# A gated attention and convolution block: ScalarE and TensorE handed to the scheduler behind the plain pairs, second-half operands emitted two products later

## The chip, the cores and the metric

The kernel runs on one core of one Trainium2 chip. The metric is the time of one execution on the device, in microseconds (us). An execution starts with all inputs in the chip's main memory and ends when the output stands there.

## What is computed

The input x is 2048 tokens by 1024 channels, float32, one layer:

```python
h    = rmsnorm(x, norm_g)
proj = h @ w_in                      # 1024 -> 6144 columns: q k v z_att B C u z_conv g_att g_conv
A    = attention(q, k, v, rel_bias)  # 8 heads of 64, own chunk of 64 and the 8 before it
ya   = (A * silu(z_att)) @ w_att_out
yc   = (B * conv3(C * u) * silu(z_conv)) @ w_conv_out
x    = x + (sigmoid(g_att) * ya + sigmoid(g_conv) * yc) @ w_out
out  = rmsnorm(x, final_norm_g)
```

## The kernel before

**Halves, pairs and products.** The projection is cut into two halves of 1024 tokens and, in each, 24 pairs of 128-column tiles. Most pairs are multiplied by a Strassen-like scheme: seven products of combined operands in place of eight, numbered 1 to 7 and taken in `ORDER` = 1, 2, 6, 5, 7, 4, 3 (line 35). Only the first half's first three pairs are multiplied plainly. The 21 pairs behind them make 147 products; this document counts them 0 to 146, and the second half's begin with 147. The last two pairs of the first half, A and B, are taken together in the order A1 A2 A6 B1 B2 B6 A5 B5 A7 B7 A4 B4 A3 B3 (products 133 to 146), the first two of the second half in the order 1 2 1 2 6 6 5 5 7 7 4 4 3 3 (products 147 to 160).

**One product.** Float32 precision comes from splitting each operand in a rounded part and its residual. A product is 12 matmuls of 128x128 by 128x512 into one PSUM bank (`passes`, lines 131 to 137): for each of four row blocks L135 (rounded weights, rounded tokens), L136 (rounded weights, token residual) and L137 (weight residual, rounded tokens). So the first matmul needs the rounded weights, and only the third needs the weight residual.

**Weights.** `operand(p, i)` makes the weights of a product: VectorE sums where the scheme wants them (L390 to L396), then `split_into`, a cast on ScalarE (L122) and the residual on VectorE (L123). The tile comes from a ring of four (`wr`), and in the first half each split weight is also stored to main memory on SyncE's queue (L399) for the second half to load (L381). A cast into a tile of the ring must wait until the product four back is done and its store has landed. `operand` is called two products ahead in the first half.

**Evictions.** Behind its matmuls a product's bank is read by VectorE (L746 to L766) or copied by ScalarE (L742), then what the pair is for follows: tanh and a store for gates (L404), a split for q and k (L410, L411), transposes on TensorE and a split for v (L433, L440, L441), SiLU for z (L453, L454). Three banks take turns.

**The second half's token operands.** `operand_steps(1)` makes them: seven steps, one for each operand number, each of four casts on ScalarE (L128, `t10h` is the rounded part of operand 1, row block 0) and four residuals on VectorE (L129), with VectorE sums ahead of some (L354, L356, L360). They go into the tiles of the first half's operands, so each step has to wait for product B of its number. In the loop a step follows product B of its number: `assert next(turned) == i` at the end of the iteration.

**What sets the order.** From the loop's start to product 160 the order of ScalarE and TensorE is the order of the program text (`tc.manual_schedule(engines=engines - {DVE})`, lines 700 and 701, closed at line 785). VectorE's order there, and every engine's later, is set by the framework's scheduler from the order in which the code emits instructions and its own estimates. Each engine then works through its instructions in that order, waiting on semaphores. DMA queues keep the order of the program.

## Time and profile before

| what | value |
|---|---|
| times of three runs | 1573.85, 1577.24 (median), 1580.59 us |
| the profiled execution | 1571.1 us, of which the profile's span is 1569.3 us |
| TensorE | busy 97% of the span |
| VectorE, ScalarE, GpSimd | 67%, 43%, 10% |
| chain that ended last | TensorE 62%, VectorE 4%, DMA 2%, ScalarE 1% |

The times of a row are microseconds from the span's start. A matmul's record is 0.39 us long though one starts every 0.23 us, since they are pipelined; what a wait costs is therefore read from starts of products. "Idle before" an instruction names what ended the wait.

### The profile page before, as it was taken

The numbers are of one execution on the slowest core, as the hardware profiler recorded it, in microseconds if no ns is written. First come the engines' busy times: TensorE is split into PE (matmuls) and PEld (weight loads), VectorE is DVE, ScalarE is ACT, GpSimd is POOL, SyncE is SP. The second block draws the span as 40 slices with busy tenths as digits, with TensorE's granted clock in tenths as the row PEclk, the third lists the DMA queues.
The fourth block names the chain that finished last, engine by engine and source line by source line (L and its number), as shares of the span: only waits on it lengthen the run. The fifth ranks groups of instructions, "written<-read, shape, count | busy, mean of one in ns | idle before, by whom it ended". The sixth has DMA issues, their size and how long they took to land.

```text
span 1569.3 us, 21720 instructions
## 1 busy us (share of the span) xinstructions
PE 1522.1 (97%) x7396; PEld 1268.2 (81%) x7396; DVE 1045.3 (67%) x2094; ACT 682.6 (43%) x1266; POOL 154.9 (10%) x294
## 2 busy tenths in 40 slices
PE   9899999999998999999999999999999999999997
PEld 6677878888786787888888888888887788888886
DVE  7978779797668653666565455446678786656544
ACT  6353343443335242333344444446666676523211
POOL 0000000000000001111121012012332222000000
PEclk9999999999999999999999999999999899999999
DMA  5287898989996926787899889898967668369231
GB/s 210 79 293 298 309 338 306 371 298 311 332 338 230 318 92 215 222 266 238 295 313 314 303 281 287 270 314 274 294 200 228 203 217 273 124 220 316 67 108 68
DMA packets 161711, 393.65 MB, mean 251 GB/s; under 512 B 20160, under 2 KB 40640, under 8 KB 161600
## 3 DMA queue, kind: packets, MB, share of 16 engines
q1 hardware_dynamic: 131392, 306.25, 56.2%
q0 software_dynamic: 20992, 69.22, 14.0%
q10 hardware_dynamic: 9216, 16.78, 2.9%
q8 instruction: 59, 0.97, 0.3%
q14 instruction: 52, 0.43, 0.1%
HBM read 241.18 MB, written 150.99 MB: 250 GB/s over the span
## 4 chain that ended last, share of the span: by engine, by line
PE 62%; DVE 4%; DMA 2%; ACT 1%; issue 1%; SPq 0%; DVEq 0%; ACTq 0%
PE ps_d L137 13%; PE ps_d L135 13%; PE ps_d L136 13%; PE ps_s L190 4%; PE po L228 4%; PE ps_d L873 3%; PE ps_d L875 3%; PE ps_d L874 3%; PE ps_t L210 3%; DMA wraw<-wy 1%; ACT pr L200 1%; DMA wraw<-wo 0%; DVE ps_s L196 0%; DVE ptl L216 0%; PE vt L433 0%
## 5 line engine op out<-in xcount | busy, mean ns | idle before, releaser
L158 POOL DMA_DIRECT2D q<-q x128 | 66.6, 526 | 710.4 <-DVE wc L123 603.3
L200 ACT ACTIVATE pr<-ps_s,nmax 128x640 f32<-128x640 f32 (+4 forms) x128 | 93.3, 729 | 89.8 <-DVE nmax L196 86.2
L196 DVE CUSTOM_DVE_ANT_0 ps_s<-ps_s,bs 128x640 f32<-128x640 f32 (+4 forms) x128 | 95.4, 745 | 48.1 <-PE ps_s L190 47.5
L215 ACT CAST pth<-ps_t 128x640 fp32r<-128x640 f32 (+4 forms) x128 | 79.8, 623 | 99.9 <-PE ps_t L210 98.5
L202 ACT ACTIVATE pr<-pr,rs 128x640 f32<-128x640 f32 (+4 forms) x128 | 97.7, 763 | 24.2 <-DVE rs L201 24.2
L190 PE MATMUL ps_s<-kk,q 128*128 128x320 f32 (+1 forms) x448 | 99.5, 336 | 8.5 <-ACT pr L200 8.3
L122 ACT CAST wc<-wraw 128x512 fp32r<-128x512 f32 x120 | 72.9, 619 | 76.5 <-DMA wc<-wc 41.6
L136 PE MATMUL ps_d<-mid,wy 128*128 128x512 f32 x256 | 101.4, 396 | 0.0
L135 PE MATMUL ps_d<-mid,wy 128*128 128x512 f32 x256 | 101.2, 395 | 0.0
L137 PE MATMUL ps_d<-mid,wy 128*128 128x512 f32 x256 | 101.2, 395 | 0.0
L216 DVE TENSOR_TENSOR ptl<-ps_t,pth 128x640 fp32r<-128x640 f32 (+4 forms) x128 | 94.2, 736 | 1.1 <-ACT pth L215 0.8
L123 DVE TENSOR_TENSOR wc<-wraw,wc 128x512 fp32r<-128x512 f32 x120 | 81.1, 688 | 12.5 <-ACT wc L122 11.5
L210 PE MATMUL ps_t<-ident,pr 128*128 128x128 f32 x560 | 84.2, 276 | 1.0 <-DVE ptl L216 0.8
L228 PE MATMUL po<-pth,vv 128*128 128x256 f32 x336 | 80.1, 272 | 2.3 <-ACT pth L215 2.2
L228 PE MATMUL po<-ptl,vv 128*128 128x256 f32 x336 | 78.5, 281 | 0.0
L190 PEld LDWEIGHTS ps_s<-kk,q 128*128 128x128 f32 x448 | 67.9, 191 | 13.0 <-ACT pr L200 12.3
L210 PEld LDWEIGHTS ps_t<-ident,pr 128*128 128x128 f32 x560 | 63.3, 140 | 11.1 <-issue 3.2
L228 PEld LDWEIGHTS po<-pth,vv 128*128 128x128 f32 x336 | 64.3, 191 | 6.8 <-ACT pth L215 3.4
L228 PEld LDWEIGHTS po<-ptl,vv 128*128 128x128 f32 x336 | 64.5, 192 | 2.7
L757 DVE TENSOR_TENSOR c<-v,ps_d 128x512 f32<-128x512 f32 x45 | 30.9, 687 | 48.7 <-PE ps_d L137 46.4
L884 ACT ACTIVATE sq<-y 128x512 f32<-128x512 f32 x32 | 20.2, 631 | 92.1 <-DVE y L879 92.0
L746 DVE TENSOR_TENSOR c<-u,ps_d 128x512 f32<-128x512 f32 x45 | 30.9, 686 | 42.3 <-PE ps_d L137 38.5
(370 smaller groups left out, 4260.0 us busy)
## 6 DMA issues: line engine op xcount, KB each, us to landing
wc<-wc SPq DMA_DIRECT2D x294, 512.0 KB, 4.7
wraw<-wp_in SPq DMA_DIRECT2D x54, 512.0 KB, 6.2
q<-q POOLq DMA_DIRECT2D x128, 128.0 KB, 4.9
gl<-gate SPq DMA_DIRECT2D x64, 256.0 KB, 3.9
mid<-mid SPq DMA_DIRECT2D x64, 256.0 KB, 5.7
bs<-bias POOLq DMA_DIRECT2D x32, 320.0 KB, 7.1
gate<-c ACTq DMA_DIRECT2D x34, 256.0 KB, 4.6
v<-vst SPq DMA_DIRECT2D x64, 128.0 KB, 4.6
```

The lines of the kernel that those rows point to most:

```text
L123: nc.vector.tensor_sub(w[:, 1], src, w[:, 0].bitcast(F32))
L135: nc.tensor.matmul(ps, lhsT=w[:, 0, k, :], rhs=rh[:, cs], start=(first and k == 0), stop=False)
L136: nc.tensor.matmul(ps, lhsT=w[:, 0, k, :], rhs=rl[:, cs], start=False, stop=False)
L137: nc.tensor.matmul(ps, lhsT=w[:, 1, k, :], rhs=rh[:, cs], start=False, stop=(last and k == len(rhs) - 1))
L190: nc.tensor.matmul(ps[:, i, :m], lhsT=q[s][:, g * P:(g + 1) * P], rhs=kk[:, k1 - n + i * m:k1 - n + (i + 1) * m], start=(s == 0), stop=(s ...
L196: nc.vector.tensor_tensor_reduce(out=view, in0=view, in1=bv, scale=-0.125, scalar=3.0e38, op0=ALU.add, op1=ALU.min, accum_out=nmax)
L200: nc.scalar.activation(out, view, AF.Exp, bias=nmax, scale=-1.0, accum_out=rs)
L202: nc.scalar.activation(pr[:, :n], pr[:, :n], AF.Identity, scale=rs)
L210: nc.tensor.transpose(out=ps[:, j * P:(j + 1) * P], in_=pr[:, j * P:(j + 1) * P], identity=ident)
L215: nc.scalar.copy(hi[:, js, qs], src)
L216: nc.vector.tensor_sub(lo[:, js, qs], src, hi[:, js, qs].bitcast(F32))
L228: nc.tensor.matmul(ps[:, (g0 + a) * P:(g0 + b) * P], lhsT=vv[:, g0 + j, :], rhs=s[:, j, a * P:b * P], start=(i == 0 and s is pt[0]), stop= ...
```

## The change

The manual order of ScalarE and TensorE behind the plain pairs is dropped, so that the scheduler orders them there as it orders VectorE. And a step of `operand_steps(1)` is no longer run at the end of the iteration s of its product B, but at the start of iteration s + 2, ahead of that iteration's weights: two products later. No arithmetic and no instruction is added or taken away.

```diff
--- before.py
+++ after.py
@@ -697,19 +697,21 @@
         scaled(*held0)
         for fn in late:
             fn()
-    manual = ExitStack()
-    manual.enter_context(tc.manual_schedule(engines=engines - {mybir.EngineType.DVE}))
     x1 = None
     nbias = 0
     att = None
     ab = None
     at_stages = 0
     turned = None
+    due = []
     uv = {}
 
     for s, (p, i) in enumerate(seq):
         half = p // NPAIR
         n = names.index(p)
+        if due and due[0] <= s:
+            due.pop(0)
+            next(turned)
         if half == 0 and i == 1 and n + 1 < NPAIR:
             for k in range(2):
                 load_raw(names[n + 1], k)
@@ -770,7 +772,7 @@
                 for _ in x1:
                     pass
                 turned = operand_steps(1)
-            assert next(turned) == i
+            due.append(s + 2)
         elif n == NPAIR + 1 + PLAIN and i == 3:
             first.close()
             att = ExitStack()
@@ -781,8 +783,6 @@
             while at_stages < min(want, 64):
                 next(ab)
                 at_stages += 1
-        if n == NPAIR + 1 and i == 3:
-            manual.close()
         if n == NPAIR + 2 + PLAIN + 8 and i == 1:
             conv_stack.close()
             gp = pool("gp", 5)
```

Three places show what it does to the order. In all of them `wc` is a product's weight tile (its number differs by two or three between the two programs).

ScalarE at the sixth gate pair, whose products are 42 to 48, before: `wc_2244` and `wc_2328` are the weights of products 43 and 46, `u_2297` is the copy of product 42's bank, `c11_2324` the tanh of product 43, L293 the squares for the second half's norm.

```order
L410 CAST hi_2241<-cv_2046 128x512
L122 CAST wc_2244<-wraw_2078 128x512
L410 CAST hi_2265<-cv_2074 128x512
L122 CAST wc_2272<-s2_2274 128x512
L742 COPY u_2297<-ps_d_2280 128x512
L122 CAST wc_2299<-s1_2273 128x512
L293 ACTIVATE xt_2214,acc_2114<-xt_2214 128x512
L293 ACTIVATE xt_2215,acc_2114<-xt_2215 128x512
L404 ACTIVATE c11_2324<-c11_2324 128x512
L405 DMA gate0_5_0_175<-c11_2324 128x512
L122 CAST wc_2328<-wraw_2080 128x512
```

and now, where `wc_2242`, `wc_2326` and `c11_2322` are the same things:

```order
L122 CAST wc_2242<-wraw_2076 128x512
L453 ACTIVATE sz_2205<-c22_2202 128x512
L122 CAST wc_2270<-s2_2272 128x512
L293 ACTIVATE xt_2212,acc_2112<-xt_2212 128x512
L453 ACTIVATE sz_2235<-u_2103 128x512
L293 ACTIVATE xt_2213,acc_2112<-xt_2213 128x512
L122 CAST wc_2297<-s1_2271 128x512
L410 CAST hi_2239<-cv_2044 128x512
L410 CAST hi_2263<-cv_2072 128x512
L744 COPY u_2295<-ps_d_2278 128x512
L122 CAST wc_2326<-wraw_2078 128x512
L404 ACTIVATE c11_2322<-c11_2322 128x512
```

The cast of product 43 stands ahead of the work of products 39 and 40 instead of behind it, and that of product 46 ahead of the tanh instead of behind it.

ScalarE in the last pair of q and k, before, from the cast of product 116 (`wc_4045`) to that of 119 (`wc_4108`); `wc_4064` is product 117's, and L410 rounds the result of product 116:

```order
L122 CAST wc_4045<-wraw_3822 128x512
L122 CAST wc_4064<-wraw_3822 128x512
L122 CAST wc_4085<-wraw_3820 128x512
L410 CAST hi_4105<-c22_4102 128x512
L122 CAST wc_4108<-wraw_3988 128x512
```

and now, where `hi_4103` is that rounding and `wc_4062` the cast of product 117:

```order
L122 CAST wc_4043<-wraw_3820 128x512
L410 CAST hi_4103<-c22_4100 128x512
L122 CAST wc_4062<-wraw_3820 128x512
L122 CAST wc_4083<-wraw_3818 128x512
L122 CAST wc_4106<-wraw_3986 128x512
```

The cast of product 117 now stands behind work on the result of product 116. In the pair behind it, the first of v (products 119 to 125), the same happens on VectorE. Before, where `wc_4226` and `wc_4250` are the weights of products 124 and 125 and `c22`, `u` (L757, L758) the evictions of product 123:

```order
L753 TENSOR_TENSOR v_4248<-u_4184,ps_d_4229 128x512
L390 TENSOR_TENSOR s1_4326<-wraw_4156 128x512
L391 TENSOR_TENSOR s2_4327<-s1_4326,wraw_4154 128x512
L396 TENSOR_TENSOR wraw_4156<-wraw_4154,wraw_4156 128x512
L123 TENSOR_TENSOR wc_4226<-wraw_3990,wc_4226 128x512
L123 TENSOR_TENSOR wc_4250<-wraw_3988,wc_4250 128x512
L441 TENSOR_TENSOR vst_4267<-vt_4242,vst_4267 128x4x64
L757 TENSOR_TENSOR c22_4273<-v_4248,ps_d_4253 128x512
L441 TENSOR_TENSOR vst_4270<-vt_4242,vst_4270 128x4x64
L758 TENSOR_TENSOR u_4184<-u_4184,ps_d_4253 128x512
```

and now (`wc_4224`, `wc_4248`; L764 is the eviction of product 124):

```order
L755 TENSOR_TENSOR v_4246<-u_4182,ps_d_4227 128x512
L390 TENSOR_TENSOR s1_4324<-wraw_4154 128x512
L441 TENSOR_TENSOR vst_4265<-vt_4240,vst_4265 128x4x64
L391 TENSOR_TENSOR s2_4325<-s1_4324,wraw_4152 128x512
L441 TENSOR_TENSOR vst_4268<-vt_4240,vst_4268 128x4x64
L396 TENSOR_TENSOR wraw_4154<-wraw_4152,wraw_4154 128x512
L759 TENSOR_TENSOR c22_4271<-v_4246,ps_d_4251 128x512
L760 TENSOR_TENSOR u_4182<-u_4182,ps_d_4251 128x512
L123 TENSOR_TENSOR wc_4224<-wraw_3988,wc_4224 128x512
L764 TENSOR_TENSOR u_4182<-u_4182,ps_d_4277 128x512
L123 TENSOR_TENSOR wc_4248<-wraw_3986,wc_4248 128x512
```

The two residuals stood ahead of the evictions of product 123; now one stands behind them and one behind that of product 124.

VectorE at the handover, before, from the weight residual of product 140 (`wc_4709`) to that of 142 (`wc_4768`):

```order
L123 TENSOR_TENSOR wc_4709<-s1_4623,wc_4709 128x512
L129 TENSOR_TENSOR t60l_4729<-xs_1596,t60h_4728 128x512
L354 TENSOR_TENSOR xs_1596<-xs_1596,xs_1602 128x512
L129 TENSOR_TENSOR t61l_4734<-xs_1596,t61h_4733 128x512
L753 TENSOR_TENSOR v_4766<-u_4559,ps_d_4751 128x512
L129 TENSOR_TENSOR t62l_4739<-xs_1596,t62h_4738 128x512
L753 TENSOR_TENSOR v_4786<-u_4649,ps_d_4772 128x512
L129 TENSOR_TENSOR t63l_4744<-xs_1596,t63h_4743 128x512
L123 TENSOR_TENSOR wc_4747<-wraw_4323,wc_4747 128x512
L123 TENSOR_TENSOR wc_4768<-wraw_4524,wc_4768 128x512
```

and now, from the residual of product 143 (`wc_4786`; that of 142, `wc_4766`, stands right ahead of it) to that of 144 (`wc_4833`):

```order
L123 TENSOR_TENSOR wc_4786<-wraw_4321,wc_4786 128x512
L759 TENSOR_TENSOR c22_4803<-v_4744,ps_d_4789 128x512
L760 TENSOR_TENSOR u_4557<-u_4557,ps_d_4789 128x512
L360 TENSOR_TENSOR t1_4809<-xs_1603,xs_1594 128x512
L454 SCALAR_TENSOR_TENSOR sz_4806<-sz_4806,c22_4803 128x512
L360 TENSOR_TENSOR t1_4815<-xs_1603,xs_1594 128x512
L129 TENSOR_TENSOR t50l_4812<-t1_4809,t50h_4811 128x512
L360 TENSOR_TENSOR t1_4821<-xs_1603,xs_1594 128x512
L129 TENSOR_TENSOR t51l_4818<-t1_4815,t51h_4817 128x512
L360 TENSOR_TENSOR t1_4827<-xs_1603,xs_1594 128x512
L129 TENSOR_TENSOR t52l_4824<-t1_4821,t52h_4823 128x512
L123 TENSOR_TENSOR wc_4833<-wraw_4522,wc_4833 128x512
```

The residuals of operand 5, which stood between the weight residuals of products 142 and 143, now stand between those of 143 and 144. On ScalarE the casts beside them are now in this order (`wc_4894` is the weight of product 146, in the ring's tile of `wc_4766`):

```order
L453 ACTIVATE sz_4806<-c22_4803 128x512
L122 CAST wc_4856<-wraw_4319 128x512
L128 CAST t50h_4811<-t1_4809 128x512
L122 CAST wc_4894<-wraw_4520 128x512
L128 CAST t51h_4817<-t1_4815 128x512
L128 CAST t52h_4823<-t1_4821 128x512
```

The cast for product 146 stands between two casts of t5, where before it followed all of t7.

## Rows read from the trace of the kernel before

**Rows 1.** Part 1 of the page, its line on all engines: busy us, share of the span, number of instructions.

```profile
PE 1522.1 (97%) x7396; PEld 1268.2 (81%) x7396; DVE 1045.3 (67%) x2094; ACT 682.6 (43%) x1266; POOL 154.9 (10%) x294
```

**Rows 2.** The waits of TensorE from 88 to 530 us of the span: who waited <- for whom, us in total, times, longest us. `ps_d L137` is the third matmul of a group, `ps_d L135` the first.

```profile
PE ps_d L137 <- DVE wc L123: 12.4, 10, 2.9
PE ps_d L135 <- ACT wc L122: 3.1, 2, 2.4
```

**Rows 3.** Busy times by stretch: start and end in us, length, then busy us (and instructions) of TensorE, of its weight loads, of VectorE, ScalarE and GpSimd, the granted clock of TensorE, the share of the DMA engines and GB/s. The stretches are the first half's products 0 to 109, products 110 to 118, to the handover, the handover, and the second half's first 30 products.

```profile
88.00:400.00 312.00, 307.74 (x1342) 251.03 (x1341) 247.91 (x447) 123.11 (x226) 0.00 (x0) 0.99 0.89 324
400.00:426.00 26.00, 22.94 (x100) 18.38 (x99) 17.50 (x28) 8.41 (x15) 0.00 (x0) 1.00 0.88 320
426.00:478.00 52.00, 52.00 (x245) 42.84 (x245) 36.61 (x65) 18.88 (x39) 0.00 (x0) 1.00 0.99 334
478.00:526.00 48.00, 39.63 (x170) 31.10 (x169) 46.01 (x78) 26.04 (x48) 0.00 (x0) 1.00 0.69 251
526.00:612.00 86.00, 86.00 (x381) 71.25 (x380) 41.64 (x63) 26.57 (x44) 6.40 (x12) 1.00 0.46 153
```

**Rows 4.** TensorE in order of time, three rows of the first half and, behind the dots, the starts of products 137 and 138: start us, us, engine, line, operation, output<-input, shape, count. `t10h` in an input means the first matmul of a product with operand 1.

```profile
90.97 0.39 PE L135 MATMUL ps_d<-t10h,wc 128*128 128x512 f32 x1
234.38 0.60 PE L91 MATMUL rb<-ident,ry 128*128 128x128 f32 x4
400.19 0.39 PE L135 MATMUL ps_d<-t40h,wc 128*128 128x512 f32 x1
...
481.34 0.39 PE L135 MATMUL ps_d<-t20h,wc 128*128 128x512 f32 x1
484.06 0.39 PE L135 MATMUL ps_d<-t60h,wc 128*128 128x512 f32 x1
```

**Rows 5.** TensorE in order of time: the first matmuls of products 42 to 47. In brackets the idle time before one, and what ended it.

```profile
206.91 0.39 PE L135 MATMUL ps_d<-t10h,wc 128*128 128x512 f32 x1
210.49 0.50 PE L135 MATMUL ps_d<-t20h,wc 128*128 128x512 f32 x1 [0.71 <-ACT wc L122]
213.74 0.39 PE L135 MATMUL ps_d<-t60h,wc 128*128 128x512 f32 x1
216.47 0.39 PE L135 MATMUL ps_d<-t50h,wc 128*128 128x512 f32 x1
221.78 0.67 PE L135 MATMUL ps_d<-t70h,wc 128*128 128x512 f32 x1 [2.43 <-ACT wc L122]
226.21 0.39 PE L135 MATMUL ps_d<-t40h,wc 128*128 128x512 f32 x1
```

**Rows 6.** ScalarE in order of time beside them: the weight cast of product 43, the tanh of a gate, and the weight casts of products 46 and 47.

```profile
209.83 0.61 ACT L122 CAST wc<-wraw 128x512 fp32r<-128x512 f32 x1
220.08 0.63 ACT L404 ACTIVATE c<-c 128x512 f32<-128x512 f32 x1 [4.76 <-DVE c L746]
221.11 1.14 ACT L122 CAST wc<-wraw 128x512 fp32r<-128x512 f32 x2 [0.40 <-ACT c L404]
```

**Rows 7.** TensorE in order of time: the third matmul of product 110, which waits, and the start of product 111.

```profile
402.33 0.50 PE L137 MATMUL ps_d<-t40h,wc 128*128 128x512 f32 x1 [1.53 <-DVE wc L123]
404.73 0.39 PE L135 MATMUL ps_d<-t30h,wc 128*128 128x512 f32 x1
```

**Rows 8.** VectorE in order of time at the start of product 110: the two evictions of product 109 and the weight residuals (`L123`) of products 110 and 111.

```profile
400.38 0.69 DVE L757 TENSOR_TENSOR c<-v,ps_d 128x512 f32<-128x512 f32 x1 [2.03 <-DMA q<-c]
400.99 0.68 DVE L758 TENSOR_TENSOR u<-u,ps_d 128x512 f32<-128x512 f32 x1
401.59 1.28 DVE L123 TENSOR_TENSOR wc<-wraw,wc 128x512 fp32r<-128x512 f32 x2
```

**Rows 9.** TensorE in order of time at the handover: the start of product 136, two of the four waits (in products 140 and 145), and the start of product 147, the second half's first.

```profile
478.62 0.39 PE L135 MATMUL ps_d<-t10h,wc 128*128 128x512 f32 x1
492.45 0.50 PE L137 MATMUL ps_d<-t50h,wc 128*128 128x512 f32 x1 [2.30 <-DVE wc L123]
513.27 0.50 PE L137 MATMUL ps_d<-t30h,wc 128*128 128x512 f32 x1 [2.94 <-DVE wc L123]
518.43 0.39 PE L135 MATMUL ps_d<-t10h,wc 128*128 128x512 f32 x1
```

**Rows 10.** VectorE in order of time at the handover: the first operand residual, the weight residual for which product 140 waits, and the first eviction of the second half.

```profile
482.68 0.69 DVE L129 TENSOR_TENSOR t10l<-xs,t10h 128x512 fp32r<-128x512 f32 x1 [1.55 <-ACT t10h L128]
491.70 0.69 DVE L123 TENSOR_TENSOR wc<-s,wc 128x512 fp32r<-128x512 f32 x1
525.16 0.69 DVE L746 TENSOR_TENSOR c<-u,ps_d 128x512 f32<-128x512 f32 x1
```

**Rows 11.** The waits of ScalarE from 88 to 478 us: its weight casts for a DMA, us in total, times, longest us.

```profile
ACT wc L122 <- DMA wc<-wc: 41.6, 24, 5.5
```

**Rows 12.** ScalarE in order of time: the weight cast of product 110.

```profile
397.20 0.62 ACT L122 CAST wc<-wraw 128x512 fp32r<-128x512 f32 x1 [3.11 <-DMA wc<-wc]
```

**Rows 13.** The weight stores (line 399) from 88 to 400 us: from issue to landing.

```profile
DMA to landing us min/median/max: 2.6/4.3/10.4
```

**Rows 14.** The same stores from 486 to 515 us.

```profile
DMA to landing us min/median/max: 2.6/3.7/5.1
```

**Rows 15.** Busy times, columns as in rows 3, of the stretch behind product 46's wait.

```profile
221.70:225.40 3.70, 3.62 (x9) 2.70 (x10) 1.89 (x3) 1.16 (x3) 0.00 (x0) 0.54 0.95 377
```

## The prediction

> **What bounds the kernel now.** First the page's line on the engines: TensorE is busy 1522.1 us of the span [rows 1]. Its queue is the clock of the whole kernel, and a change of order can only win what it waits. Then its waits in the part that the change touches, from 88 to 530 us: nearly all are third matmuls held up by a weight residual of VectorE (12.4 us in 10 waits) and first matmuls held up by a weight cast of ScalarE (3.1 us in 2) [rows 2]. The stretches show where they lie: some in the long quiet part, about 3 us between 400 and 426 us, and most at the handover, where VectorE is busy 46.01 of 48 us; the second half's first products run without a gap [rows 3].
>
> The cost of a wait is read from starts of products, since a matmul's record overlaps the next. Undisturbed, one product follows another by 484.06 − 481.34 = 2.72 us [rows 4]. Product 0 starts at 90.97 and product 110 at 400.19: 309.22 us for 110 × 2.72 = 299.2 us of work and two groups of transposes of about 0.36 us (the group recorded at 234.38 and one like it) [rows 4]. So the quiet part loses 309.2 − 299.2 − 0.7 = **9.3 us**. The largest pieces are products 42 and 43, 213.74 − 206.91 − 5.44 = 1.4 us, and products 45 and 46, 226.21 − 216.47 − 5.44 = 4.3 us [rows 5]. Products 110 and 117 each wait 1.53 us; 110 takes 404.73 − 400.19 = 4.54 us, so it loses 1.8 us [rows 7], and the two together **3.7 us** (of the 3.06 us idle in their stretch [rows 3] the rest is pipeline refill). The handover, products 136 to 146, takes 518.43 − 478.62 = 39.8 us for 11 × 2.72 = 29.9 us [rows 9]: **9.9 us** lost. All of it is 22.9 us.
>
> **Part 1: ScalarE out of program order, the quiet part.** At products 43 and 46 the weight cast is late because program order puts it behind other work: the cast at 209.83 behind the gated result's rounding, the casts at 221.11 behind a tanh that waited 4.76 us for VectorE [rows 6]. In the new order both casts stand ahead of that work, as the order of ScalarE shows. The waits for residuals in this part (products 5, 16, 22, 58, 85 and smaller ones) come where VectorE has a residual behind an eviction and several more instructions; in the new order, for products 0 to 109, a residual stands next to an eviction at least two products old or further back. How much slack that leaves: residual row start to third matmul is 402.33 − 401.59 = 0.74 us, an eviction starts 400.38 − 400.19 = 0.19 us behind the next product's start and takes 0.61 us to the next instruction [rows 7, 8]; so a residual right behind the eviction of two products ago has its third matmul ready 0.19 + 0.61 + 0.74 = 1.54 us after the start of the product ahead, and it is due 2.72 + 0.45 us after it. I take the whole 9.3 us as gained. The bounds: half of it (4.7 us), if ScalarE's casts meet late stores where VectorE's order shows nothing, and all of it.
>
> TensorE's own order hardly changes: two pairs of products are interleaved (136 with 137, 142 with 143) and one group of transposes fills a wait. Dropping its manual order costs and gives nothing by itself; the matmuls are the same.
>
> **Part 2: products 111 to 125.** Product 110's residual now stands ahead of the evictions of product 109, so its 1.8 us go; nothing is late behind it. Product 117 gets worse. Its cast stands behind the rounding of product 116's result: eviction at 0.19, rounding from 0.88 (0.69 us behind, [rows 8]), cast from 1.45, done at 2.07 us after the product is due; VectorE's residual follows at 2.2 and the third matmul at 2.94 in place of 0.45: it loses 2.5 us, with the slower restart (the matmul after a wait takes 0.34 us) 2.6. Products 124 and 125 are new: 124's residual stands behind both evictions of product 123, the same order that cost product 110 1.8 us; 125's behind one eviction, 0.61 us sooner, and transposes fill 0.36 us of that wait: 1.53 − 0.45 − 0.36 + 0.1 = 0.8 us. Together 2.6 + 1.8 + 0.8 = 5.2 against 3.7: **1.5 us lost**. Bounds: 0.5 (the hole of 117 as it was) and 3.
>
> **Part 3: the handover.** VectorE is the limit there: from 482.68 to 525.16 us it runs one instruction per 0.60 us without a gap [rows 10], so a residual's time is found by counting the rows ahead of it. Times from the start of product 136, in the new order:
> - Product 136: its residual stands behind the eviction of product 135 (0.19): it starts at 0.79, its third matmul at 1.53; two matmuls of product 137 go first, so it was due at 0.91. Lost 0.6.
> - VectorE then waits for the first casts of operand 1, whose tile is free when product 136's third matmul is done (1.92); by the chain of casts and residuals the residual of product 138 starts at 5.0, and from there nothing holds VectorE up.
> - Product 142: its residual is 24 rows behind that of 138: 5.0 + 24 × 0.60 = 19.4, the third matmul 20.15. Due: 6 × 2.72 + 0.6 + 0.9 = 17.85. Lost 2.3.
> - Product 144: 12 rows on, 26.6. But ScalarE's cast for product 146 stands between two casts of operand 5, and it needs the ring's tile of product 142, whose store can only start at 20.1. Stores there landed in 2.6 to 5.1 us, median 3.7 [rows 14]; with 3.7 (and 0.35 us to issue) the cast starts at 24.2, the next operand cast ends at 25.3, and VectorE's order slips by 0.6: residual 27.2, third matmul 27.9, due 25.1. Lost 2.8 (2.2 with a landing of 2.6, 4.2 with 5.1).
> - Product 149 needs the bank of product 146, whose eviction is 23 instructions behind the residual of 144: done 41.7, due 41.1. Lost 0.6. Later steps of the operands (4 and 3) have over 10 us to spare, and the second half's loads stay ahead.
>
> The sum is 6.3, with four restarts of 0.1 us 6.8, against 9.9: **3.1 us gained**. Bounds: −1 (the longest landing, and the loads of products 148 and 149, which SyncE's queue now issues behind a store that waits for VectorE, 2 us late) and +5. A sentence on the skill: the Trainium skill, DMA: Bandwidth & Descriptors, section on the anatomy of one DMA, gives about 2 us fixed plus bytes over 436 GB/s, an estimate of 3.2 us for these 512 KB; by it product 144 would lose 2.3 us and the sum would be 0.5 us better. The rows' 3.7 us are used.
>
> Behind product 149 all engines keep their order, so the rest of the kernel moves as a whole.
>
> **The sum.** 9.3 − 1.5 + 3.1 = 10.9 us. The profiled execution took 1571.1 us, 0.4% below the median of the runs; 1571.1 − 10.9 = 1560.2, and from the median 1577.24 − 10.9 = **1566.3 us**.
>
> **The rivals.**
> *The clock falls in the new waits (same).* Behind the 2.43 us wait of product 46 the clock was granted at 0.54 over 3.7 us, mostly the level of 1.2 GHz [rows 15], matmuls took 0.67 us [rows 5], and the product lost 4.43 − 2.72 = 1.7 us more. Against it: behind waits of 2.30 and 2.94 us at the handover [rows 9] the stretch's clock stayed at 1.00 [rows 3]. Should it fall behind products 117, 142 and 144, that is 3 × 1.7 = 5.1 us: gain 5.8, 1571.4 us. The Trainium skill, TensorE: Matmul & The Clock Gate, section on loop structure, has matmuls run cold behind a wait; the trace shows both. Chance 0.12.
>
> *The quiet part keeps half its waits (same).* The ring of four ties a cast to a store; ScalarE waited 41.6 us for stores in 24 casts [rows 11], and the scheduler's estimate of a store may be short. 4.7 instead of 9.3, and a long landing at product 146's cast (1.4): gain 4.8, 1572.4 us. For it: stores that took up to 10.4 us [rows 13]. Chance 0.22.
>
> *The ring closes (slower).* Product 110's cast waited 3.11 us for its store and ended at 397.82, 2.4 us ahead of its product [rows 7, 12]. A cast that stands further ahead holds everything behind it on ScalarE until the store has landed: copies of banks, roundings, tanh. In the 21 pairs of the first half this decides if the landings grow by more than those 2.4 us over the median of 4.3 [rows 13]: at 8.0 each pair would lose 1.3 us, 27 us in all, net 16 us slower, 1593 us. Against it: the stores themselves start earlier when residuals do. Chance 0.11.
>
> **How the numbers follow.** Forecast 0.52 (1566.3; its own range from the bounds of parts 2 and 3: gains of 9.3 − 3 − 1 = 5.3 and 9.3 − 0.5 + 5 = 13.8 us, 1563.4 to 1571.9), a handover without any loss 0.03 (9.3 − 1.5 + 9.9 = 17.7, 1559.5), the rivals 0.12, 0.22 and 0.11. A measurement of this kernel can tell 0.5%, 7.9 us, from no change. Faster by more: 0.52 + 0.03 = 0.55; same 0.12 + 0.22 = 0.34; slower 0.11. The range goes from the better handover to both rivals near no change together (4.8 − 5.1, about 0: 1577), and leaves out the slower case: 1559 to 1577.
>
> **What would show it.** Right: no wait of TensorE between 91 and 390 us over 0.5 us; products 110 to 125 with holes at 117, 124 and 125; four holes at products 136, 142, 144 and 149 that sum to some 7 us, VectorE without a gap; product 147's start some 11 us earlier against product 0's. Wrong: casts of ScalarE that wait for stores while TensorE stands still in the quiet part, a granted clock below 1 behind product 117 or 144, or a handover that again loses 10 us.

## The result and the profile after

The changed kernel took **1566.8 us** (median of 6 runs, 1562.5 to 1569.8) against 1577.6 us before (6 runs): a ratio of **0.9936**, interval 0.9910 to 0.9962. The forecast was 1566.3 us. In a second set of runs it took 1569.2 us (12 runs) against 1574.0 (15 runs; one more, of 5379 us, was in a slower state and is left out): 0.9960, interval 0.9941 to 0.9979. So the gain is under 2%, but clear of noise in both sets. The medians differ by 10.7 us in the first and 4.8 us in the second; the two intervals together reach from 3 to 14 us. The forecast's 10.9 us is the gain of the first set, and the sections below show what can take the difference.

The profiled execution took 1562.5 us, its span is 1560.6. From the page, the engines' line, which answers to [rows 1]:

```profile
PE 1516.7 (97%) x7396; PEld 1266.2 (81%) x7396; DVE 1043.2 (67%) x2094; ACT 686.5 (44%) x1266; POOL 154.8 (10%) x294
```

The waits of TensorE from 88 to 530 us, as in [rows 2] (who waited <- for whom, total us, times, longest):

```profile
PE ps_d L137 <- DVE wc L123: 5.1, 4, 2.7
PE ps_d L135 <- ACT wc L122: 3.5, 3, 1.9
```

12.4 us of waits for residuals have become 5.1. The busy times of the same stretches as in [rows 3] (start and end, length, busy us of TensorE, weight loads, VectorE, ScalarE, GpSimd, granted clock, DMA share, GB/s):

```profile
88.00:400.00 312.00, 312.00 (x1381) 258.13 (x1380) 253.22 (x459) 130.32 (x233) 0.00 (x0) 1.00 0.91 333
400.00:426.00 26.00, 23.97 (x105) 19.20 (x104) 16.44 (x26) 7.92 (x15) 0.00 (x0) 1.00 0.95 333
426.00:478.00 52.00, 49.76 (x231) 39.92 (x230) 35.66 (x64) 19.77 (x41) 0.00 (x0) 1.00 0.88 299
478.00:526.00 48.00, 43.64 (x183) 34.83 (x182) 43.05 (x71) 23.40 (x41) 0.00 (x0) 0.96 0.83 285
526.00:612.00 86.00, 85.42 (x378) 70.37 (x377) 41.78 (x65) 27.41 (x46) 7.58 (x14) 1.00 0.48 161
```

In the first stretch TensorE no longer waits at all (before: 307.74 of 312 us, at a clock of 0.99). Two stretches have other waits than before: 400 to 426 us, where product 110's is gone and product 117's is longer, and 426 to 478 us, which had none. TensorE in order of time shows them, at products 117, 124 and 125 (start, us, engine, line; in brackets the idle time and what ended it):

```profile
412.36 0.50 PE L135 MATMUL ps_d<-t40h,wc 128*128 128x512 f32 x1 [1.95 <-ACT wc L122]
434.52 0.50 PE L137 MATMUL ps_d<-t40h,wc 128*128 128x512 f32 x1 [1.53 <-DVE wc L123]
438.46 0.50 PE L137 MATMUL ps_d<-t30h,wc 128*128 128x512 f32 x1 [0.49 <-DVE wc L123]
```

and ScalarE at the first of them:

```profile
411.17 0.62 ACT L410 CAST hi<-c 128x512 fp32r<-128x512 f32 x1 [7.01 <-DVE c L759]
411.70 1.66 ACT L122 CAST wc<-wraw 128x512 fp32r<-128x512 f32 x3
```

ScalarE stood idle for 7 us ahead of the rounding of product 116's result, until VectorE had made that result, and three weight casts, product 117's first, came only behind it. At the handover, TensorE in order of time: products 136 and 142 (first matmul, then its third), 144's third matmul, and the starts of 145, 146 and 147:

```profile
471.39 0.50 PE L135 MATMUL ps_d<-t10h,wc 128*128 128x512 f32 x1 [0.23 <-ACT wc L122]
489.56 0.50 PE L135 MATMUL ps_d<-t70h,wc 128*128 128x512 f32 x1 [1.31 <-ACT wc L122]
491.19 0.50 PE L137 MATMUL ps_d<-t70h,wc 128*128 128x512 f32 x1 [0.39 <-DVE wc L123]
499.15 0.50 PE L137 MATMUL ps_d<-t40h,wc 128*128 128x512 f32 x1 [2.67 <-DVE wc L123]
...
502.36 0.63 PE L135 MATMUL ps_d<-t30h,wc 128*128 128x512 f32 x1
...
505.90 0.40 PE L135 MATMUL ps_d<-t30h,wc 128*128 128x512 f32 x1
...
508.63 0.39 PE L135 MATMUL ps_d<-t10h,wc 128*128 128x512 f32 x1
```

The wait of product 142's first matmul goes back to ScalarE's casts for products 142 to 144, which waited for a VectorE sum (L396) that stood among the operand rows:

```profile
488.89 1.66 ACT L122 CAST wc<-wraw 128x512 fp32r<-128x512 f32 x3 [0.65 <-DVE wraw L396]
```

Behind the longest wait stand ScalarE's cast for product 146 and VectorE's residual behind the next cast:

```profile
495.42 0.62 ACT L122 CAST wc<-wraw 128x512 fp32r<-128x512 f32 x1 [1.23 <-DMA wc<-wc]
```

```profile
496.60 0.69 DVE L129 TENSOR_TENSOR t51l<-t,t51h 128x512 fp32r<-128x512 f32 x1 [0.65 <-ACT t51h L128]
```

This is the chain that the prediction described: cast waits for the store of product 142's weight, VectorE waits for the next cast, and product 144's residual, three rows behind the one shown, is late.

All kernels of this study are compared by the starts of products. Lost time is the difference of two starts less 2.72 us per product and 0.36 us per group of transposes. "Rest" is from product 313's start to the end of the span. Each row is one execution; two executions of one kernel differ in a column of lost time by up to 2.8 us, and by product 313 by up to 4.0.

| kernel | lost 0–109 | 110–132 | 133–146 | 147–181 | product 0 to 313 | rest |
|---|---|---|---|---|---|---|
| before | 9.3 | 4.3 | 10.4 | 0.0 | 969.1 | 509.2 |
| before, again | 8.1 | 4.3 | 13.2 | 0.0 | 970.1 | 510.5 |
| the change | 0.3 | 5.8 | 8.1 | 0.0 | 958.8 | 510.8 |
| the change, again | 0.3 | 7.3 | 9.0 | 1.5 | 962.8 | 510.8 |
| E1 steps early | 0.3 | 5.8 | 7.3 | 2.5 | 961.6 | 515.0 |
| E2 steps late, order written | 9.2 | 4.3 | 16.5 | 0.0 | 974.4 | 516.8 |
| E3 ScalarE alone written | 7.6 | 4.3 | 15.3 | 0.2 | 971.8 | 514.9 |
| E4 sums on GpSimd | 0.3 | 7.1 | 12.4 | 6.2 | 971.0 | 514.6 |
| E5 steps when due | 0.3 | 7.2 | 1.8 | 1.9 | 956.8 | 514.7 |
| E6 operand 5 later | 0.3 | 5.8 | 3.5 | 6.0 | 961.3 | 515.7 |
| E7 VectorE written 111–132 | 0.3 | 2.6 | 7.0 | 0.0 | 954.6 | 515.0 |
| E8 both, 111–136 | 0.3 | 2.7 | 2.1 | 0.4 | 951.4 | 514.6 |
| E9 both, 111–123 | 0.3 | 1.3 | 0.4 | 4.6 | 951.1 | 516.2 |
| E10 E9 and stores aside | 0.3 | 1.1 | 0.4 | 0.8 | 946.9 | 511.4 |

The rest, in which every compute engine's order is the same in all these kernels, takes 509 to 517 us; why it differs is not shown. It is a reason why single times say less than the products, and why the profile's 8.6 us of gain (1571.1 − 1562.5) are less than the 10.4 us gained by product 313: the first profile of before had the shortest rest of all.

### The profile page after: what moved, and what is told of

It is laid out like the page before. It is cut to its first block, busy times and chain, and to the rows that moved or that the text cites. A ratio compares the mean times of both kernels' runs of the same rounds, so it can differ in the third digit from the quotient of the medians.

```text
span 1560.6 us, 21691 instructions
## 1 busy us (share of the span) xinstructions
PE 1516.7 (97%) x7396; PEld 1266.2 (81%) x7396; DVE 1043.2 (67%) x2094; ACT 686.5 (44%) x1266; POOL 154.8 (10%) x294
## 4 chain that ended last, share of the span: by engine, by line
PE 83%; DVE 7%; DMA 6%; ACT 2%; issue 2%; SPq 0%; ACTq 0%; DVEq 0%
PE ps_d L137 20%; PE ps_d L135 20%; PE ps_d L136 20%; PE ps_s L190 4%; PE po L228 4%; PE ps_d L875 3%; PE ps_d L874 3%; PE ps_d L873 3%; PE ps_t L210 3%; DMA wraw<-wy 2%; DMA mid<-mid 1%; DMA wraw<-wo 1%; DVE xs L304 1%; DMA wc<-wc 1%; DMA gate<-u 1%
## 5 line engine op out<-in xcount | busy, mean ns | idle before, releaser
L137 PE MATMUL ps_d<-mid,wy 128*128 128x512 f32 x256 | 101.0, 394 | 0.4 <-DVE wy L123 0.4
L135 PE MATMUL ps_d<-mid,wy 128*128 128x512 f32 x256 | 101.1, 395 | 0.0
L123 DVE TENSOR_TENSOR wc<-wraw,wc 128x512 fp32r<-128x512 f32 x120 | 82.1, 689 | 13.1 <-ACT wc L122 13.0
L190 PEld LDWEIGHTS ps_s<-kk,q 128*128 128x128 f32 x448 | 68.0, 191 | 13.0 <-ACT pr L200 12.4
L210 PEld LDWEIGHTS ps_t<-ident,pr 128*128 128x128 f32 x560 | 63.3, 140 | 11.6 <-issue 3.7
L755 DVE TENSOR_TENSOR v<-u,ps_d 128x512 f32<-128x512 f32 x45 | 30.9, 688 | 45.1 <-PE ps_d L137 44.5
```

The lines of the kernel that those rows point to most:

```text
L123: nc.vector.tensor_sub(w[:, 1], src, w[:, 0].bitcast(F32))
L135: nc.tensor.matmul(ps, lhsT=w[:, 0, k, :], rhs=rh[:, cs], start=(first and k == 0), stop=False)
L137: nc.tensor.matmul(ps, lhsT=w[:, 1, k, :], rhs=rh[:, cs], start=False, stop=(last and k == len(rhs) - 1))
L190: nc.tensor.matmul(ps[:, i, :m], lhsT=q[s][:, g * P:(g + 1) * P], rhs=kk[:, k1 - n + i * m:k1 - n + (i + 1) * m], start=(s == 0), stop=(s ...
L210: nc.tensor.transpose(out=ps[:, j * P:(j + 1) * P], in_=pr[:, j * P:(j + 1) * P], identity=ident)
```

## The experiments

**Theory:** what TensorE loses is set by which rows stand ahead of a weight cast on ScalarE or a weight residual on VectorE; the free order clears the quiet part, and at the handover the operand rows that stand ahead of residuals cost. **Rivals:** the later emission alone shortens the handover; VectorE simply has too much to do there; the ring and its stores set it.

### The two parts of the change apart

E1: the free order with the step where it was.

```diff
-            due.append(s + 2)
+            next(turned)
```

> ScalarE and TensorE free, but each operand step emitted where it was before, at the end of the iteration of its product B. Theory (free order brings the quiet part, the later emission only the handover): products 0 to 109 lose under 0.6 us as with the whole change, products 110 to 125 lose 5.3 us as there, and the handover (products 136 to 146) loses 8.2 to 9.9 us in place of 7.9, since the weight residuals of products 142 and 144 stand two VectorE rows (1.2 us) further back and product 136 is no longer late (0.9). Rival (the later emission carries the handover's gain alone): 9.9 us as before. Rival (both parts are needed everywhere): the quiet part loses several us again.

Products 0 to 125 repeat the change's. Products 136 to 146 lose 6.5 us, less than the expected 8.2 to 9.9 (product 136 is late by the same 0.9 us, so that is not the later emission's doing), but the second half's start then loses 2.5 (the first matmuls of products 148 and 149 wait for their loads):

```profile
512.02 0.47 PE L135 MATMUL ps_d<-t20h,wc 128*128 128x512 f32 x1 [1.51 <-DMA wc<-wc]
515.41 0.47 PE L135 MATMUL ps_d<-t10h,wc 128*128 128x512 f32 x1 [0.39 <-DMA wc<-wc]
```

9.7 us from product 133 to 181, between the change's 8.1 and its second profile's 10.5. So the gain is nearly all the free order's; whether the later emission adds anything to it stays open within these 2 us.

E2: the other part alone, the written-out order kept. Against the kernel before, the lines that fill and empty `due` come in as in the change; of them here:

```diff
-            assert next(turned) == i
+            due.append(s + 2)
```

> The written-out order of ScalarE and TensorE kept, operand steps emitted two products later. Theory (ScalarE's order sets the quiet part): products 0 to 109 lose 9.3 us and products 110 to 125 3.7 us, all as before the change; at the handover the weight residual of product 144 stands 35 VectorE rows behind an eviction in place of 29, and I expect 10 to 12 us lost in place of 9.9. Rival (the later emission itself shortens the handover): 7.9 us or less lost there, total gain 2 us.

The quiet part and products 110 to 132 are as before, as the theory wants. The handover is far worse than expected: 15.4 us at products 136 to 146. Its third matmuls in products 144 and 146 wait again, and their longer records show the slow clock:

```profile
511.95 0.79 PE L137 MATMUL ps_d<-t40h,wc 128*128 128x512 f32 x1 [1.65 <-DVE wc L123]
521.86 0.79 PE L137 MATMUL ps_d<-t30h,wc 128*128 128x512 f32 x1 [2.74 <-DVE wc L123]
```

Part of this is the clock's price. The rival on later emission falls: by itself it costs 4 to 5 us by product 313 (974.4 us against 969.1 and 970.1).

E3: later emission, ScalarE alone written out (against E2).

```diff
-    manual.enter_context(tc.manual_schedule(engines=engines - {mybir.EngineType.DVE}))
+    manual.enter_context(tc.manual_schedule(engines={mybir.EngineType.Activation}))
```

> Operand steps two products later, only ScalarE's order written out, TensorE's free. Theory (TensorE's order costs and gives nothing by itself; VectorE's order follows ScalarE's): as the run with both engines written out, product by product within 0.5 us: 9.3 us lost up to product 109, 3.7 us at 110 to 125, 10 to 12 us at the handover. Rival (TensorE's free order, with products 136 and 137 interleaved, is a part of the gain): 1 to 3 us less lost at the handover than with both written out.

The same holes stay; ScalarE's written order is what keeps them. But TensorE's freedom is not worth nothing here: 1.6 us less in the quiet part than E2, where TensorE now puts matmuls of the next product into a wait. The 1.2 us less at the handover are within what the clock changes there from one execution to the next.

### Is VectorE's total work the limit of the handover?

E4: the 12 sums of the second half's operands on GpSimd.

```diff
-                    nc.vector.tensor_add(b11[:, j, :], b11[:, j, :], b12[:, j, :])
+                    (nc.gpsimd if half else nc.vector).tensor_add(b11[:, j, :], b11[:, j, :], b12[:, j, :])
...
```

> The whole change, and the 12 sums of the second half's operands (L354, L356, L360) on GpSimd, which is idle there: 12 rows of 0.60 us, 7.2 us of VectorE's work at the handover, go. Theory A (the rows that stand ahead of a weight residual on VectorE set the handover): products 136 to 146 lose 1 to 3 us in place of 7.9, total 5 to 7 us less than the change. Theory B (the ring's tile and its store set it): product 144 still loses 2 us or more, 5 to 7 us in all. No row shows such a sum on GpSimd; if it took over 2 us, 8 us for a step's four, the casts behind it would be late, VectorE would stand behind their residuals, and the handover would lose as much as now or more, 8 to 15 us.

Slower: products 136 to 146 lose 11.6 us, inside the 8 to 15 of the third case, though a sum took less than the 2 us named there. GpSimd in order of time (the four sums of operand 4, the first three of operand 5's four):

```profile
488.74 6.55 POOL L356 TENSOR_TENSOR xs<-xs 128x512 f32<-128x512 f32 x4 [2.58 <-DMA z<-sz]
495.26 5.08 POOL L360 TENSOR_TENSOR t<-xs 128x512 f32<-128x512 f32 x3
```

and VectorE beside them:

```profile
489.04 0.68 DVE L755 TENSOR_TENSOR v<-u,ps_d 128x512 f32<-128x512 f32 x1
489.63 1.18 DVE L129 TENSOR_TENSOR t22l<-xs,t22h 128x512 fp32r<-128x512 f32 x1
490.74 1.75 DVE L129 TENSOR_TENSOR t23l<-xs,t23h 128x512 fp32r<-128x512 f32 x1
492.40 1.74 DVE L123 TENSOR_TENSOR wc<-wraw,wc 128x512 fp32r<-128x512 f32 x1
```

A sum costs about 1.65 us on GpSimd, and a VectorE row that reads both operands from SBUF beside it (the last two shown) takes 1.75 us in place of 0.69. VectorE lost its sums, but its other rows grew longer. This decides nothing between the theories.

E5 asks the same without GpSimd: each step emitted shortly ahead of its first use.

```diff
+NPAIR = 24; LATER = {1: 2, 2: 3, 6: 6, 5: 7, 7: 8, 4: 8, 3: 8}
...
-            due.append(s + 2)
+            due.append(s + LATER[i])
```

> The whole change, but each operand step emitted only a little ahead of its first use: 2, 3, 6, 7, 8, 8, 8 products behind its product B in place of 2 for all. Theory A (what costs at the handover is which VectorE rows stand ahead of a weight residual): residuals of products 142 and 144 lose the 8 to 16 operand rows ahead of them, products 136 to 146 lose 1 to 3 us in place of 7.9 (0.9 of it at product 136, which stays), and products 147 to 160 under 1.5 us. Theory B (VectorE has too much to do at the handover, whatever the order): the same 40 rows, 24 us, only move the loss: products 136 to 160 lose 6 to 8 us in all. Up to product 135 nothing differs from the change.

Products 136 to 146 lose 1.0 us (7.3 in the change). The stretch, columns as in [rows 3]:

```profile
478.00:526.00 48.00, 46.09 (x203) 37.54 (x202) 45.69 (x76) 25.54 (x46) 0.00 (x0) 1.00 0.91 322
```

VectorE is as busy as before the change, 45.69 against 46.01 us [rows 3], and busier than in the change (43.05), while TensorE has 46.09 us against 39.63 and 43.64. Products 136 to 160 lose 2.9 us, where theory B wanted 6 to 8, and it falls: **a nearly full VectorE did not bound the handover; the order of its rows did.** The 1.8 us behind product 148 (expected: under 1.5) were a first matmul waiting for a load.

E6 moves one step only.

```diff
-            due.append(s + 2)
+            due.append(s + (4 if i == 5 else 2))
```

> The whole change, with one step alone, that of operand 5, two products later still (four behind its product B). Its eight VectorE rows then stand behind the weight residuals of products 144 to 146 and its casts behind the cast of product 146. Theory A (order): product 144's hole (3.8 to 5.5 us with what the clock adds) goes, that of product 142 (2.3) and 136 (0.9) stay: the handover loses 3.0 to 3.6 us in place of 7.9 or 8.8. Theory B (total work): what product 144 wins, products 145 to 150 lose again.

Product 144's hole is gone and those of 136 and 142 stay: products 135 to 146 lose 3.2 us, inside the expected 3.0 to 3.6. So the eight rows of operand 5 and the cast between them were that hole, as the prediction had it. The ring alone does not make it: the cast for product 146 still waits for its store, and nothing is late behind it.

```profile
495.02 0.62 ACT L122 CAST wc<-wraw 128x512 fp32r<-128x512 f32 x1 [1.97 <-DMA wc<-wc]
```

But products 148 and 149 then lose 5.9 us, as much as theory B wanted, though not by its cause: the first matmul of product 149 waits for its load, and SyncE's queue issues that load (the first in the last row) behind a store of z, 5 us after product 145, whose tile it needs, was done (500.8 us).

```profile
513.34 0.47 PE L135 MATMUL ps_d<-t10h,wc 128*128 128x512 f32 x1 [4.03 <-DMA wc<-wc]
```

```profile
505.34 0.32 SPq L460 DMA_DIRECT2D z<-sz  x1
505.70 0.43 SPq L373 DMA_DIRECT2D wraw<-wp_in  x1
506.23 0.87 SPq L381 DMA_DIRECT2D wc<-wc  x2
```

That store waited for L454 of VectorE (504.63 us), which now stands behind the rows of operand 5. So the order of VectorE's rows came back by another way; E10 takes the queue out of it.

### The new holes at products 117, 124 and 125

E7: VectorE in program order for these iterations.

```diff
-        half = p // NPAIR
+        half = p // NPAIR; s == 111 and written.enter_context(tc.manual_schedule(engines={mybir.EngineType.DVE})); s == 133 and written.close()
```

> The whole change, but VectorE in program order for the iterations of products 111 to 132. There a weight residual stands ahead of the evictions of the product two before its own. Theory (the holes at 117, 124 and 125 are rows that stand ahead of a cast or a residual): products 110 to 125 lose under 0.6 us in place of 5.3, the rest is as in the change: about 5 us less at product 133. Rival (the casts are late because the ring's tile waits for its store, and the scheduler was right to put other work first): VectorE then stands still behind such a residual, its evictions come late, and the stretch loses 3 us or more.

The three holes are gone: products 110 to 125 lose 0.7 us in place of 5.4. A new hole of 1.5 us opens behind product 126, whose copied bank the next first matmul waits for:

```profile
442.14 0.50 PE L135 MATMUL ps_d<-t20h,wc 128*128 128x512 f32 x1 [1.12 <-ACT u L744]
```

3 us gained of the expected 5. What the rival described does happen: between 400 and 442 us ScalarE's weight casts waited 9.4 us for stores, and VectorE stood still behind such casts (who waited <- for whom, total us, times, longest):

```profile
DVE wc L123 <- ACT wc L122: 7.1, 6, 1.6
```

In the change it did so once, for 0.6 us. But TensorE lost only 0.7 us up to product 125, so the rival's price, 3 us or more, did not come.

### The parts together

E8: E5, and VectorE in program order for products 111 to 136 (E7's line, closed at 137).

> Both together: steps emitted when due, and VectorE in program order for the iterations of products 111 to 136. By theory A products 0 to 109 lose 0.4 us, 110 to 135 under 0.8, 136 to 160 under 2.5: 9 to 12 us less than the change, 19 to 21 less than before at product 313; median 1554 to 1559 us, ratio to before 0.986 to 0.989. By theory B (VectorE's total at the handover) 5 us less than the change, 1562 us, ratio 0.990.

1556.8 us (median of 6), ratio **0.9884** (0.9855 to 0.9914). From product 0 to 313 it takes 951.4 us, 17.7 less than before; the expected 19 to 21 were cut by the holes behind product 126 and at product 133 (1.5 and 1.9 us). Products 136 to 146 lose nothing measurable (0.0 us) any more. The handover's stretch:

```profile
478.00:526.00 48.00, 47.84 (x211) 39.34 (x210) 44.57 (x75) 22.95 (x41) 0.00 (x0) 1.00 0.86 314
```

E9: the same, closed at 124 instead of 137.

> As the run with both, but VectorE in program order only for the iterations of products 111 to 123, so that the transposes of v and the evictions behind them are the scheduler's again. Theory (the 1.4 us at product 126 and 1.7 us at product 133 of that run come from copies on ScalarE that stand behind splits of transposed banks, which program order on VectorE had put there): both go, products 110 to 135 lose under 1 us in place of 4.8 less the transposes' 1.9; 2 to 3 us less at product 313 than the run with both; median 1552 to 1556 us, ratio 0.986 to 0.989. Rival (the holes at 126 and 133 come with the residuals ahead of the transposes' splits in 111 to 123): product 126 loses 1.4 us again.

Both holes go, and products 110 to 146 lose 1.7 us in place of 4.8. But the time stays: 1558.3 us, 0.9873 (0.9838 to 0.9907), where 1552 to 1556 was expected. What was won is lost at products 148 and 149 (4.6 us), again to a load. SyncE's queue in order of time shows why:

```profile
494.65 0.38 SPq L381 DMA_DIRECT2D wc<-wc  x1
497.24 0.32 SPq L460 DMA_DIRECT2D z<-sz  x1
497.61 0.92 SPq L373 DMA_DIRECT2D wraw<-wp_in  x2
498.64 1.15 SPq L381 DMA_DIRECT2D wc<-wc  x2
```

The load of product 149, the first in the last row, needs product 145's tile, free at 495.1 us. But it stands behind a store of z that waits 2 us for VectorE, and behind two raw weights, and is issued at 498.64.

E10: E9 with the first half's stores of z on GpSimd's queue.

```diff
-            defer(1, lambda: store(z_d[pr][g], t))
+            defer(1, lambda: (nc.gpsimd.dma_start if g < 2 else store)(z_d[pr][g], t))
```

> As the shorter run with both, and the first half's stores of z (L460) on GpSimd's queue in place of SyncE's. There the loads of the second half's weights (L381) stood behind these stores, which wait for L454 of VectorE; the load of product 149 was issued at 498.6 us though product 145, whose tile it needs, was done at 495.1, and product 149 began 3.0 us late behind it. Theory (SyncE's order is the next limit): the load is issued 2 us or more sooner against product 145's end, and products 147 to 150 lose 0 to 2.5 us in place of 4.5; 2 to 4 us less at product 182; median 1553 to 1557 us. Rival (the transfers themselves are the limit there, two raw weights of 512 KB and the loads sharing the DMA engines): the load lands no sooner and 4 to 5 us are lost there again, median 1556 to 1560 us.

The load is now issued 0.2 us behind product 145's end (495.86 us):

```profile
494.99 0.32 SPq L399 DMA_DIRECT2D wc<-wc  x1
495.36 0.46 SPq L373 DMA_DIRECT2D wraw<-wp_in  x1
496.06 5.76 SPq L381 DMA_DIRECT2D wc<-wc  x3
```

and products 147 to 181 lose 0.8 us in place of 4.6. So most of the loss was the queue's order: the load is issued 3.3 us sooner against product 145's end. The transfers are the rest: the load itself takes 8.5 us to land, in E9 7.6. By the products it is the shortest kernel of all, 946.9 us, 22 less than before; by its runs (1557.4 us, just above the expected 1553 to 1557; 0.9877, interval 0.9846 to 0.9909) it can't be told from E8 and E9. All three beat the change and the kernel before.

### Both kernels again

> The kernel before, a second profile. Theory (its holes belong to its order, their length only partly to the clock and to landings): products 0 to 109 lose 9 to 10 us, 110 and 117 1.8 us each, the handover 9 to 11 us, from product 0 to 313 within 2 us of the first profile's 969.2 us. Rival (the holes are luck, the first profile was one draw): they stand at other products, and the stretch differs by over 4 us.

The holes stand at the same products, though two sums miss what was expected. The quiet part lost 8.1 us (the clock fell less behind product 46: 0.4 us lost there in place of 1.7), the handover (136 to 146) 12.7: product 145 waited 2.92 us, as in the first profile (2.94 [rows 9]), but this time the clock fell behind it. TensorE's third matmul of product 145, and the busy times around it (columns as in [rows 3]):

```profile
513.27 0.79 PE L137 MATMUL ps_d<-t30h,wc 128*128 128x512 f32 x1 [2.92 <-DVE wc L123]
```

```profile
512.00:518.60 6.60, 5.33 (x13) 4.17 (x14) 6.60 (x13) 1.90 (x4) 0.00 (x0) 0.55 1.07 372
```

Products 145 and 146 lost 5.35 + 0.85 us where the first profile had 3.35: a price of 2.9 us. By product 313 the two profiles differ by 0.9 us.

> The change itself, a second profile. Theory (what differs behind the last product, 509.2 us before and 510.9 us after from the start of product 313 to the end, is transfers' luck and no part of the change): the starts of products 0 to 313 repeat within 0.3 us, 10.4 us ahead of before at product 313, and the rest takes anything from 509 to 517 us, as it did in the other four programs. Rival (the change has made the rest 1.7 us longer): it takes 510.9 us again within 0.5. The median of the runs: 1564 to 1569 us.

The rest took 510.8 us again, as the rival had it, but the kernel before took 510.5 in its second profile. So neither luck nor a longer rest is shown. The median, 1569.2 us, is just above the expected range. The starts did not repeat within 0.3 us: products 0 to 313 took 4.0 us longer. Three places hold it: product 117 (1.4 us), products 144 and 145 (1.0) and the start of product 149 (1.4). At 117 the wait is the same 1.95 us in both executions, and what follows is not. The granted clock of product 117 in the first profile and in the second (columns as in [rows 3]):

```profile
412.36:415.57 3.21, 3.13 (x12) 2.29 (x13) 1.36 (x3) 0.99 (x2) 0.00 (x0) 1.00 0.66 262
```

```profile
414.86:419.50 4.64, 4.61 (x12) 3.34 (x13) 1.35 (x3) 1.09 (x2) 0.00 (x0) 0.63 0.81 307
```

At 144 it was the store: ScalarE's cast for product 146 waited 2.22 us in place of 1.23, and TensorE 3.66 in place of 2.67. At 149 the first matmul waited:

```profile
520.33 0.47 PE L135 MATMUL ps_d<-t10h,wc 128*128 128x512 f32 x1 [1.19 <-DVE sz L454]
```

The row names a VectorE instruction whose result this product does not use. The bank of product 146 had been read by 517.9 us; the load of product 149's weights was issued at 513.49, behind a store of z, and landed 6.7 us later, at 520.2.

## Why the prediction was right, and where it was not

**Part 1, the quiet part: right.** 9.3 us forecast, 9.0 gained (309.22 us from product 0 to 110 [rows 4], now 300.25). No wait is left there. The rival by which half the waits stay (gain 4.8) is out, and so is the closing ring.

**TensorE's order "costs and gives nothing": wrong as a general statement.** With ScalarE written out it gave 2.6 us by product 313 (E3 against E2), 1.6 of them in the quiet part; with ScalarE free it was not tried.

**Part 2, products 110 to 125: right to 0.1 us a hole in the first profile.** 117 lost 2.6 (forecast 2.6), 124 lost 1.8 (1.8), 125 lost 0.9 (0.8): together 5.3 against 5.2. They were read by counting rows and adding three row lengths. In the second profile 117 lost 4.0, by the clock.

**Part 3, the handover: mechanism right, one term too small.** Products 135 to 146 lost 7.8 us. The forecast for them is 6.0: its four terms with their restarts are 0.7, 2.4, 2.9 and 0.7, which is 6.7 and not the 6.8 written, and the last is product 149's. Product 136: 0.9 (0.7), of which 0.5 was a first matmul that waited for its cast. 142: 2.3 (2.4). Here too the first matmul waited longest, 1.31 us for a cast, which the prediction did not list; it cost nothing more, since the residual's matmul came 20.3 us behind the start of product 136, where 20.15 was worked out. 144: the third matmul came at 499.15, 28.3 us behind the undelayed start of product 136 (470.9), where 27.9 was worked out, and the wait itself cost 3.0 (2.9). What the sum left out is the clock behind it: from that matmul to product 145 it took 502.36 − 499.15 = 3.21 us, where product 110 took 2.40 [rows 7], and product 145 lost 0.82 with matmuls of 0.63 us: together **1.6 us**, nearly the 1.7 that the first rival had put on such a fall. Product 149 (0.6 forecast, by product 146's bank) began on time in this execution and 1.4 us late in the second. There its load was what it waited for, which the prediction had among its bounds, not in its sum; so this term had the wrong cause.

**The clock rival came true in part.** It had a chance of 0.12 for all three places at once. In fact the waits do not go together: in the first profile the clock fell behind 144 and not behind 117, in the second behind both. That, a longer landing and product 149 are what lies between a gain of 10.4 and one of 6.4 us by product 313. It would have been better to put about half of 1.7 us on each new wait of some 2 us or more, an estimate from the 3 falls in 6 executions at product 117.

**The sum.** 10.9 us forecast; 10.4 by product 313 in the first profile and 6.4 in the second, 10.7 between the medians of the first set of runs and 4.8 in the second. The forecast time was hit in the first set, to 0.5 us, which is partly luck, since the sum left out 1.6 us of clock and two executions of the kernel differ by 4.0 us by product 313. 1569.2 us of the second lies inside the range too. "The rest moves as a whole" held in the first profile up to product 181; beyond 313 executions differ by up to 8 us.

## What to carry to other kernels

In a kernel whose bound engine waits for two others, find for each wait the instruction that ends it, and count the rows that stand ahead of that on its own engine; this gave the holes at products 117, 124, 125 and 142 and the wait at 144 to 0.1 us, but not what the clock adds behind one. A helper engine that is 95% busy is not thereby the limit: rows needed over 20 us later stood ahead of rows needed now, and emitting each step when it is due freed 6 us of the handover without taking a row away (2 of them were lost again to a load). When a hole closes, look at once for what feeds the products behind it: here loads in a queue behind a store that waited for VectorE took most of the gain back until the store went elsewhere.

## What the runs showed of the hardware

A granted clock of 1.00 is TensorE's level of 2.4 GHz, 0.50 that of 1.2 GHz, and a figure between them is a stretch with both. Behind one and the same wait it is not one value: after 1.95 us of waiting at product 117 it stayed at 1.00 in three executions (the change, E1, E6), and product 117 lost 0.5 us, and fell to 0.62 to 0.63 in three others (the change again, E4, E5), where it lost 1.7 to 1.9. In the three where it stayed, product 0 began at 90.5 to 91.0 us of the span, in the others at 92.3 to 93.5. Before the change, behind product 145's wait of 2.9 us, it stayed at 1.00 in one execution [rows 3, 9] and was 0.55 in the other, which lost 2.9 us more; both waits ended at 513.27 us of the span. So the moment in the span alone does not decide, and what does is not shown. A fall cost 1.3 to 2.9 us. The Trainium skill, TensorE: Matmul & The Clock Gate, section on the HAM clock gate, says of a kernel's start that the same kernel shows different numbers of cold matmuls from run to run; these traces show such a difference in the middle of the kernel.

A VectorE row with both inputs in SBUF took 1.74 to 1.77 us where GpSimd sums ran beside it all the time and 0.68 otherwise, while an eviction that reads PSUM and SBUF (L755) kept its 0.68 us beside one (E4). The Trainium skill, SBUF — State Buffer, section "Who interferes with whom", states this: a VectorE instruction with two SBUF inputs contends with a GpSimd instruction that reads SBUF, one with at most one such input, outside the two-port modes, does not. The rows agree on both halves.
